# Attention heads of a hybrid decoder trunk: scaling and row minima inside the score instruction, a Newton step on ScalarE, fp32 sums of squares, and the second half of the keys' rows by DMA

## The chip, the cores and the metric

One NeuronCore of a Trainium2 chip runs the kernel: TensorE (PE) for matmuls, VectorE (DVE), ScalarE (ACT) and GpSimd (POOL) for elementwise work, SyncE (SP) for issuing most DMAs. Each engine works through its own queue in order and waits on semaphores for the others. The metric is device time in microseconds (us) of one execution; a comparison takes the median of several runs.

## The reference, cut to what matters

The trunk has one convolution layer, one differential-attention layer and a final RMSNorm, over 16 meta tokens and 1024 tokens of width 1024. All tensors are float32. The change lies in the attention layer, which has 8 heads, each with two query/key pairs of width 64 and values of width 128:

```python
for i in range(n_blocks):                       # blocks of 128 queries
    s = einsum("bqhmd,bkhmd->bhmqk", q[i], k[:qe]) * scale
    alibi = -slopes[:, None, None] * abs(qpos - kpos)
    s = where(valid, s + alibi[:, None], NEG_BIG)
    p = softmax(s, axis=-1)
    a = p[:, :, 0] - lam * p[:, :, 1]
    outs.append(einsum("bhqk,bkhe->bqhe", a, v))
o = rms_norm(o, subln_gain) * (1.0 - lambda_init)
o = o.reshape(b, l, DIFF_WIDTH) * silu(z)
return einsum("blc,cd->bld", o, w_out)
```

## The kernel before

The kernel keeps float32 accuracy on matmuls of a faster type: every operand is split into a high part (fp32r) and a low part, and a product is made of three passes, high by high, high by low and low by high. ACT casts the high part and DVE or POOL subtracts to get the low one (`lo_part`, L158). `passes` (L208) issues the matmuls of all projections.

The program runs in stages: norm, convolution with its two projections, second norm, values, then the eight heads, then the output projection and final norm. The order of each engine's instructions is not written by hand: a scheduler with a simulated timeline of its own sets it from the order of the code and the buffers that come free. So work of head h+1 (its projections `q`, `k` and `za`) stands between the attention work of head h on PE.

`queries(h)` makes `q2`: for each of the two pairs m, 64 rows of high parts and in the other 64 rows the low parts, so that one matmul of 128 rows gives both products with a key that stands twice. `keys(h)` therefore makes `k2[m]` and `kl2[m]` (high and low part of the keys, 1040 columns) with the same 64 rows in both halves: DVE scales the projection (`kt`, L889), ACT casts (L892), POOL subtracts (L158) and POOL copies both parts to the other 64 rows (L893 and L897), chunk by chunk (three chunks of some 347 columns).

`attention(h)` goes over four output quarters j of 256 queries, each of two blocks i of 128. For each block and each m the scores of up to 1040 keys come in one to three chunks: two matmuls into a score bank (L954, L955; three banks), then one DVE instruction (L957) that adds the distances `base`, writes `p` and gives the least value of the chunk to a column of `st`. The scores are held negated and divided by the head's slope. A DVE instruction or two (L962, L964, L968) take the least of the chunks and multiply by the slope; ACT then makes the exponential with scale -slope and that bias, and its row sum (L969); DVE the reciprocal (L973). For the second of the pair `st` is multiplied by -lambda (L976). ACT scales p0 (L982), DVE adds p1 times its factor (L983), PE transposes (L993), ACT and DVE split the result (L997, L998) and PE multiplies with the values into the one output bank `oo`.

Per quarter a norm follows: ACT squares the output (`osq`, L1023); for heads 0 to 3 (`SOH` = 4) the squares are split (L1028, `sr`) and summed by two fp32r matmuls with ones (L1031), for heads 4 to 7 by one fp32 matmul (L1033), into the second half of the output bank (`so`). ACT makes exp(-0.5 ln(so/128 + eps)) (L1035, L1036), DVE makes a Newton step for it (L1037, L1039, L1040, L1041), POOL one product (L1038); the result is split and stored by SP (`ya_d`).

SP's queue holds the loads of weights (`wf`, L174), those stores and, near the end of the heads, the loads of the residual (`f`, L1142), which go into buffers of the ring `qk` that held queries and keys of head 6. Work buffers of the norm (`sq`, `y`, `x`, `r`) come from a ring of four, `sm`.

## Time and profile before

| | us |
|---|---|
| median of 3 runs | 1518.32 |
| lowest and highest run | 1514.34, 1518.41 |
| the profiled execution's own time | 1522.14 |
| its span, first to last instruction | 1520.4 |
| PE busy in the span | 1430.9 (94%) |
| DVE busy | 1214.4 (80%) |
| POOL busy | 999.1 (66%) |
| ACT busy | 876.4 (58%) |

Busy time is a share over stages of different kinds, so one reads it by stretch. A matmul's record overlaps the next one's, so busy PE time includes some in which PE could have done more. In rows of groups the first number after the bar is busy time in us, the second the mean of one instruction in ns; behind the second bar stands the idle time of the engine just before such instructions and what ended it. In a row of a timeline or of the chain the first number is the start, the second the length.

### The profile page before, as it was taken

Reading aid. Unit: us, or ns where it says so; the run is one execution under the profiler, and the core shown is the slowest. Engines: PE = TensorE matmul, PEld = TensorE weight load, DVE = VectorE, ACT = ScalarE, POOL = GpSimd, SP = SyncE. Lnnn points to the kernel's source line nnn. Section 1 sums busy time; section 2 is a strip of 40 time slices with the busy share of each in tenths; the row PEclk is TensorE's granted clock in tenths of the full one; section 3 lists DMA queues with packets and bytes.
Section 4 is the critical chain, followed back from the end, with each engine's and each line's share of the span. In section 5 each row is a group of like instructions: output and inputs, shape, how many; then the busy total and the mean of one; then the engine's idle time right before and its main releaser. Section 6 shows DMA issues by size and latency. Waiting matters only on the chain.

```text
span 1520.4 us, 24170 instructions
## 1 busy us (share of the span) xinstructions
PE 1430.9 (94%) x8794; PEld 1332.9 (88%) x8794; DVE 1214.4 (80%) x2285; ACT 876.4 (58%) x1552; POOL 999.1 (66%) x782
## 2 busy tenths in 40 slices
PE   7799999999999988899999999989999999999887
PEld 6799999999999988799998878878888888887787
DVE  8999999989999988868445311689899898888784
ACT  5566666665655637546324412557768677687451
POOL 6599999999999973435014502947477485685572
PEclk9999999999999998899999999999999999999999
DMA  5021111112111313644453633111211212146541
GB/s 176 28 70 42 56 49 63 57 42 70 51 48 49 112 50 112 196 138 148 152 170 124 205 99 105 42 42 61 81 49 61 85 38 74 56 136 220 175 142 65
DMA packets 77369, 142.31 MB, mean 94 GB/s; under 512 B 6465, under 2 KB 45890, under 8 KB 76226
## 3 DMA queue, kind: packets, MB, share of 16 engines
q1 hardware_dynamic: 62242, 114.49, 23.1%
q0 software_dynamic: 5728, 17.04, 3.6%
q10 hardware_dynamic: 9280, 9.23, 1.8%
q8 instruction: 69, 1.13, 0.3%
q14 instruction: 50, 0.41, 0.1%
HBM read 106.73 MB, written 34.01 MB: 93 GB/s over the span
## 4 chain that ended last, share of the span: by engine, by line
PE 36%; DVE 24%; POOL 18%; ACT 10%; issue 8%; DMA 3%; SPq 0%; POOLq 0%; DVEq 0%; ACTq 0%
POOL pb L500 14%; PE c L208 8%; PE v L208 6%; PE z L208 5%; PE ao L208 3%; PE k L208 3%; PE u L208 3%; DVE p L957 3%; ACT pr L499 2%; DVE p L983 2%; ACT p L969 2%; PE q L208 2%; DVE v L534 2%; PE za L208 2%; PE g L208 1%
## 5 line engine op out<-in xcount | busy, mean ns | idle before, releaser
L500 POOL TENSOR_TENSOR pb<-pr,pb 128x521 f32<-128x521 f32 (+1 forms) x272 | 387.8, 1435 | 15.7 <-ACT pr L499 1.1
L499 ACT ACTIVATE pr<-vr,chn 128x521 f32<-128x521 f32 x224 | 150.7, 724 | 115.3 <-POOL pb L500 114.6
L208 PE MATMUL c<-b,wh 128*128 128x260 f32 x1024 | 190.5, 288 | 6.5 <-DVE b L158 3.9
L190 ACT ACTIVATE wh<-wf 128x1024 fp32r<-128x1024 f32 x115 | 121.0, 1052 | 105.7 <-PE c L208 51.3
L513 DVE SCALAR_TENSOR_TENSOR ev<-vr,chn,ev 128x520 f32<-128x520 f32 x240 | 180.7, 753 | 1.3
L208 PEld LDWEIGHTS c<-b,wh 128*128 128x128 f32 x1024 | 162.1, 193 | 7.7 <-DVE b L158 4.8
L208 PE MATMUL g<-hp,wh 128*128 128x346 f32 (+1 forms) x752 | 149.5, 329 | 13.7 <-DVE sig L467 6.0
L158 DVE TENSOR_TENSOR wl<-wf,wh 128x1024 fp32r<-128x1024 f32 x81 | 128.8, 1590 | 37.9 <-ACT wh L190 37.8
L208 PE MATMUL u<-hp,wh 128*128 128x346 f32 (+1 forms) x752 | 149.7, 321 | 3.5 <-ACT sz L432 2.1
L208 PE MATMUL c<-b,wl 128*128 128x260 f32 x512 | 146.5, 288 | 5.2 <-DVE wl L158 5.2
L969 ACT ACTIVATE p<-p,st 128x144 f32<-128x144 f32 (+7 forms) x128 | 100.5, 785 | 76.0 <-DVE st L964 41.8
L208 PEld LDWEIGHTS g<-hp,wh 128*128 128x128 f32 x752 | 125.8, 192 | 18.4 <-ACT n_r L233 6.3
L208 PE MATMUL z<-hp,wh 128*128 128x346 f32 (+1 forms) x768 | 136.2, 322 | 1.9 <-ACT sig L464 1.9
L513 DVE SCALAR_TENSOR_TENSOR od<-xs,wc,od 128x520 f32<-128x520 f32 x176 | 132.1, 751 | 0.0
L208 PEld LDWEIGHTS u<-hp,wh 128*128 128x128 f32 x752 | 124.5, 188 | 4.8 <-ACT sz L432 2.4
L208 PEld LDWEIGHTS z<-hp,wh 128*128 128x128 f32 x768 | 124.7, 189 | 2.7 <-ACT sig L464 2.2
L957 DVE CUSTOM_DVE_ANT_0 p<-s,total 128x144 f32<-128x144 f32 (+6 forms) x224 | 108.2, 500 | 13.1 <-PE s L955 10.0
L158 POOL TENSOR_TENSOR wl<-wf,wh 128x1024 fp32r<-128x1024 f32 x34 | 83.9, 2467 | 45.5 <-ACT wh L190 31.7
L208 PEld LDWEIGHTS c<-b,wl 128*128 128x128 f32 x512 | 98.8, 193 | 6.1 <-DVE wl L158 5.8
L667 POOL TENSOR_TENSOR total<-hsq,total 128x520 f32<-128x520 f32 x12 | 21.1, 1757 | 117.5 <-ACT hsq L666 117.5
L954 PE MATMUL s<-k,q 128*128 128x256 f32 (+6 forms) x224 | 76.8, 348 | 8.9 <-DVE st L957 8.7
L208 PE MATMUL z<-hp,wl 128*128 128x346 f32 (+1 forms) x384 | 74.2, 325 | 11.2 <-DVE wl L158 11.2
(300 smaller groups left out, 3723.2 us busy)
## 6 DMA issues: line engine op xcount, KB each, us to landing
wf<-conv_in SPq DMA_DIRECT2D x48, 512.0 KB, 3.4
wf<-conv_out SPq DMA_DIRECT2D x32, 512.0 KB, 3.8
wf<-attn_in SPq DMA_DIRECT2D x32, 512.0 KB, 3.5
wf<-attn_out SPq DMA_DIRECT2D x17, 512.0 KB, 3.5
sz_d<-sz ACTq DMA_DIRECT2D x32, 260.0 KB, 4.0
szr<-sz_d SPq DMA_DIRECT2D x16, 520.0 KB, 4.2
v<-v_d POOLq DMA_DIRECT2D x8, 1024.0 KB, 5.6
ya_d<-yb SPq DMA_DIRECT2D x28, 256.0 KB, 2.5
```

The costliest lines, as they stand in the source:

```text
L158: return eng.tensor_tensor(out=out_, in0=full, in1=hi, op=ALU.subtract)
L190: A.activation(out=wh, in_=wf, func=AF.Copy)
L208: PE.matmul(o, a[k], b[k], start=start and i == 0, stop=stop and i == tot - 1)
L499: A.activation(out=d, in_=src, func=AF.Copy, scale=w)
L500: G.tensor_tensor(out=dst, in0=d, in1=dst, op=ALU.add)
L513: V.scalar_tensor_tensor(out=dst, in0=src, scalar=w, in1=dst, op0=ALU.mult, op1=ALU.add)
L534: eng.tensor_tensor(out=v_t[i], in0=v_t[i], in1=mean, op=ALU.subtract)
L667: (V if SQA[m] == "V" else G).tensor_tensor(out=total[:, ns], in0=sq, in1=total[:, ns], op=ALU.add)
L954: PE.matmul(o[:, :wm], q2[m][:, qs], k2[m][:, c0 : c0 + wm], start=True, stop=False)
L957: V.tensor_tensor_reduce(out=p[:, c0 : c0 + w], in0=o[:, :w], in1=base[:, t0 + c0 : t0 + c0 + w], scale=1.0, scalar=0.0, op0=ALU.add, op1= ...
L969: A.activation(out=p[:, :n], in_=p[:, :n], func=AF.Exp, scale=-slope, bias=st[:, 0:1], accum_out=st[:, 1:2],)
L983: V.scalar_tensor_tensor(out=p0[:, :n], in0=p1[:, :n], scalar=s1[:, 3:4], in1=p0[:, :n], op0=ALU.mult, op1=ALU.add)
```

## The change

It touches only the heads.

- The score instruction takes the slope as its scale and, for the second and third chunk of a tile, the least value of the chunk before as its start value (3e38 for the first). So the last chunk's least value is that of the tile, already scaled, and the exponential uses scale -1 and it as bias. The small instructions in between are gone.
- The product with -lambda is a tensor_scalar with a scalar from memory in place of a tensor_tensor.
- In the Newton step, -0.5 so/128 - 0.5 eps is made by ACT (Identity with a bias tile), ACT squares r into a new buffer `rr` of the ring `sm`, and DVE multiplies once.
- `SOH` is 0: all heads sum the squares with one fp32 matmul.
- The keys' other 64 rows are written by four DMAs per head on SP's queue (64 x 1040 float32 each), issued after all three chunks, in place of POOL's copies per chunk.

```diff
@@ -60,7 +60,7 @@
 LOV = [(0, 2, 4, 6)] * 3
 SR = "G"
 SOE = "V"
-SOH = 4
+SOH = 0
 AGATE = [(7, 0)] * 3 + [(7, 1)] * 4
 AQ = "GGGGGGG"
 DIR0 = (False, False, False)
@@ -151,6 +151,8 @@
     V.memset(zero, 0.0)
     eps = gp.tile([P, 1], F32, name="eps")
     V.memset(eps, EPS)
+    half_eps = gp.tile([P, 1], F32, name="half_eps")
+    V.memset(half_eps, -0.5 * EPS)
     mod = gp.tile([P, KD, 3], F32, name="mod")
     sub_g = gp.tile([P, 1], F32, name="sub_g")
 
@@ -888,15 +890,14 @@
                 t = ev(f"kt{h}_{c0}")[:, :w]
                 V.tensor_tensor(out=t, in0=o, in1=rst[:, cs], op=ALU.mult)
                 for m in range(2):
-                    ms, other = slice(64 * m, 64 * m + 64), slice(64 - 64 * m, 128 - 64 * m)
+                    ms = slice(64 * m, 64 * m + 64)
                     A.activation(out=k2[m][ms, cs], in_=t[ms], func=AF.Copy)
-                    G.tensor_scalar(
-                        out=k2[m][other, cs], in0=k2[m][ms, cs].bitcast(F32), scalar1=1.0, scalar2=None, op0=ALU.mult
-                    )
                     lo_part(V if KL == "V" else G, kl2[m][ms, cs], t[ms], k2[m][ms, cs].bitcast(F32))
-                    G.tensor_scalar(
-                        out=kl2[m][other, cs], in0=kl2[m][ms, cs].bitcast(F32), scalar1=1.0, scalar2=None, op0=ALU.mult
-                    )
+
+            for m in range(2):
+                ms, other = slice(64 * m, 64 * m + 64), slice(64 - 64 * m, 128 - 64 * m)
+                for t in (k2[m], kl2[m]):
+                    SP.dma_start(out=t[other].bitcast(F32), in_=t[ms].bitcast(F32))
             return k2, kl2
 
         def gate(h):
@@ -947,33 +948,28 @@
                     for m in range(2):
                         p = pt(f"p{h}_{i}_{m}")
                         st = gp.tile([P, 8], F32, tag="stat", name=f"st{h}_{i}_{m}", bufs=6)
-                        mins = []
-                        for c0, w in even_chunks(n):
+                        least = 3e38
+                        for ci, (c0, w) in enumerate(even_chunks(n)):
                             wm = max(w, 256)
                             o = score(f"s{h}_{i}_{m}_{c0}")
                             PE.matmul(o[:, :wm], q2[m][:, qs], k2[m][:, c0 : c0 + wm], start=True, stop=False)
                             PE.matmul(o[:, :wm], q2[m][:, qs], kl2[m][:, c0 : c0 + wm], start=False, stop=True)
-                            mins.append(st[:, 4 + len(mins) : 5 + len(mins)])
+
                             V.tensor_tensor_reduce(
-                                out=p[:, c0 : c0 + w], in0=o[:, :w], in1=base[:, t0 + c0 : t0 + c0 + w], scale=1.0,
-                                scalar=0.0, op0=ALU.add, op1=ALU.min, accum_out=mins[-1],
+                                out=p[:, c0 : c0 + w], in0=o[:, :w], in1=base[:, t0 + c0 : t0 + c0 + w], scale=slope,
+                                scalar=least, op0=ALU.add, op1=ALU.min, accum_out=st[:, 4 + ci : 5 + ci],
                             )
-                        if len(mins) == 3:
-                            V.tensor_tensor(out=mins[1], in0=mins[1], in1=mins[2], op=ALU.min)
-                        if len(mins) > 1:
-                            V.tensor_scalar(
-                                out=st[:, 0:1], in0=mins[0], scalar1=mins[1], scalar2=slope, op0=ALU.min, op1=ALU.mult
-                            )
-                        else:
-                            V.tensor_scalar(out=st[:, 0:1], in0=mins[0], scalar1=slope, scalar2=None, op0=ALU.mult)
+                            least = st[:, 4 + ci : 5 + ci]
                         A.activation(
-                            out=p[:, :n], in_=p[:, :n], func=AF.Exp, scale=-slope, bias=st[:, 0:1],
+                            out=p[:, :n], in_=p[:, :n], func=AF.Exp, scale=-1.0, bias=least,
                             accum_out=st[:, 1:2],
                         )
                         V.reciprocal(out=st[:, 2:3], in_=st[:, 1:2])
                         pr.append((p, st))
                     (p0, s0), (p1, s1) = pr
-                    SMALL[SE].tensor_tensor(out=s1[:, 3:4], in0=s1[:, 2:3], in1=neg_lam, op=ALU.mult)
+                    V.tensor_scalar(
+                        out=s1[:, 3:4], in0=s1[:, 2:3], scalar1=neg_lam, scalar2=None, op0=ALU.mult
+                    )
                     if i in PSC:
                         G.tensor_scalar(
                             out=p0[:, :n], in0=p0[:, :n], scalar1=s0[:, 2:3], scalar2=None, op0=ALU.mult
@@ -1034,10 +1030,12 @@
                 x, r = small(f"ox{h}_{j}", w=256), small(f"or{h}_{j}", w=256)
                 A.activation(out=r, in_=so, func=AF.Ln, scale=1.0 / P, bias=eps)
                 A.activation(out=r, in_=r, func=AF.Exp, scale=-0.5)
-                V.tensor_scalar(out=x, in0=so, scalar1=-0.5 / P, scalar2=-0.5 * EPS, op0=ALU.mult, op1=ALU.add)
                 pool_ops[h, j] = G.tensor_tensor(out=y, in0=y, in1=r, op=ALU.mult).ins
-                V.tensor_tensor(out=x, in0=x, in1=r, op=ALU.mult)
-                V.tensor_tensor(out=x, in0=x, in1=r, op=ALU.mult)
+
+                A.activation(out=x, in_=so, func=AF.Identity, scale=-0.5 / P, bias=half_eps)
+                rr = small(f"rr{h}_{j}", w=256)
+                A.activation(out=rr, in_=r, func=AF.Square)
+                V.tensor_tensor(out=x, in0=x, in1=rr, op=ALU.mult)
                 V.scalar_tensor_tensor(out=y, in0=x, scalar=1.5, in1=y, op0=ALU.add, op1=ALU.mult)
                 if h == HEADS - 1 and j < 2:
                     if j == 0:

```

The scheduler sets a new order in the heads; up to there it is the same. Three places show it (line numbers of the changed kernel differ by a few from those before: its score instruction is L958, its key transfer L900). The first is DVE in head 3, around the seventh of eight blocks (`p3_6_0`, `p3_6_1`: probabilities of pair 0 and 1; `st`: their columns of least values, sums and factors). Before:

```order
L957 ISA p3_6_0_11730,st3_6_0_11731<-s3_6_0_456_11736,total_6321 128x456
L957 ISA st3_6_0_11731 128x1
L973 RECIPROCAL st3_5_1_11652<-st3_5_1_11652 128x1
L964 TENSOR_SCALAR st3_6_0_11731<-st3_6_0_11731 128x1
L976 TENSOR_TENSOR st3_5_1_11652<-st3_5_1_11652,neg_lam_8209 128x1
L983 SCALAR_TENSOR_TENSOR p3_5_0_11638<-p3_5_1_11651,st3_5_1_11652,p3_5_0_11638 128x784
L973 RECIPROCAL st3_6_0_11731<-st3_6_0_11731 128x1
L957 ISA p3_6_1_11743,st3_6_1_11744<-s3_6_1_0_11745,total_6321 128x456
L957 ISA st3_6_1_11744 128x1
L957 ISA p3_6_1_11743,st3_6_1_11744<-s3_6_1_456_11749,total_6321 128x456
L957 ISA st3_6_1_11744 128x1
```

Now:

```order
L958 ISA p3_6_0_11589,st3_6_0_11590<-s3_6_0_456_11595,total_6323,st3_6_0_11590 128x456
L958 ISA st3_6_0_11590 128x1
L994 TENSOR_TENSOR atl3_2_0_11460<-tp3_4_0_11490,ath3_2_0_11458 128x4x128
L958 ISA p3_6_1_11601,st3_6_1_11602<-s3_6_1_0_11603,total_6323 128x456
L958 ISA st3_6_1_11602 128x1
L994 TENSOR_TENSOR atl3_2_1_11461<-tp3_4_1_11497,ath3_2_1_11459 128x2x128
L958 ISA p3_6_1_11601,st3_6_1_11602<-s3_6_1_456_11607,total_6323,st3_6_1_11602 128x456
L958 ISA st3_6_1_11602 128x1
L967 RECIPROCAL st3_6_0_11590<-st3_6_0_11590 128x1
```

The multiplications with the slope (L964) are gone, and the second chunk's instruction reads `st`, which the first chunk's accumulator row wrote.

The second place is PE at the start of head 0, where the first scores (`s0_0_0_0`: head 0, block 0, pair 0) follow the key projection (`k0_2`); `q1_0` and `q1_1` are the two chunks of head 1's query projection. Before:

```order
L208 MATMUL k0_2_9138<-g7_8028,wl82_8358 128x346
L954 MATMUL s0_0_0_0_9181<-k0_0_9058,q0_0_8353 128x256
L208 MATMUL q1_0_9671<-g0_7172,wh83_9064 128x512
L208 MATMUL q1_0_9671<-g1_7293,wh83_9064 128x512
L954 MATMUL s0_0_1_0_9190<-k1_0_9059,q1_0_8354 128x256
L954 MATMUL s0_1_0_0_9208<-k0_0_9058,q0_0_8353 128x272
```

Now:

```order
L210 MATMUL q1_1_9666<-g1_7295,wh83_9066 128x512
L955 MATMUL s0_0_0_0_9175<-k0_0_9060,q0_0_8355 128x256
L210 MATMUL q1_1_9666<-g2_7417,wh83_9066 128x512
L210 MATMUL q1_1_9666<-g3_7540,wh83_9066 128x512
L955 MATMUL s0_0_1_0_9183<-k1_0_9061,q1_0_8356 128x256
L955 MATMUL s0_1_0_0_9200<-k0_0_9060,q0_0_8355 128x272
```

The first scores stood at place 5082, right behind the key projection; now they stand at 5116, behind 34 matmuls of head 1's query projection.

The third place is SP near the end of head 6 (`ya_d`: stores of finished quarters; `f`: residual loads; `wf`: weights). Before:

```order
L174 DMA wf105_14804<-attn_out 128x1024
L1052 DMA ya_d_8234<-yb5_3_13322 256x1x256
L1142 DMA f2_14783<-h1_d_76 128x1024
L1142 DMA f3_14784<-h1_d_76 128x1024
L1142 DMA f4_14785<-h1_d_76 128x1024
L1142 DMA f5_14786<-h1_d_76 128x1024
L1052 DMA ya_d_8234<-yb6_0_13661 256x1x256
```

Now:

```order
L1050 DMA ya_d_8236<-yb5_3_13128 256x1x256
L1050 DMA ya_d_8236<-yb6_0_13456 256x1x256
L1140 DMA f2_14545<-h1_d_78 128x1024
L1140 DMA f3_14546<-h1_d_78 128x1024
L900 DMA k0_7_13903<-k0_7_13903 64x1040
L900 DMA k1_7_13904<-k1_7_13904 64x1040
L1140 DMA f4_14547<-h1_d_78 128x1024
L900 DMA kl0_7_13905<-kl0_7_13905 64x1040
L900 DMA kl1_7_13906<-kl1_7_13906 64x1040
L176 DMA wf106_14595<-attn_out 128x1024
```

The four transfers of head 7's keys stand behind the first two residual loads and around the third; on PE, 23 matmuls of the gate projection, 19 of head 6's output and 8 transposes stand between head 6's last score matmul and head 7's first.

## Rows read from the trace of the kernel before

**Rows 1.** Stretches of the heads: start and end, length, busy time by engine, PEclk, DMA

```profile
943.00:1029.70 86.70, 80.87 (x462) 72.02 (x461) 60.16 (x195) 51.61 (x115) 62.68 (x61) 0.98 0.13 40
1029.70:1389.70 360.00, 345.54 (x2017) 306.67 (x2017) 320.98 (x939) 257.90 (x548) 245.04 (x239) 0.99 0.26 86
1389.70:1430.00 40.30, 36.27 (x179) 30.07 (x179) 36.29 (x90) 27.24 (x49) 17.61 (x15) 0.96 0.40 123
```

**Rows 2.** Timeline of ACT, one load per head: start, length, instruction

```profile
1029.74 1.28 ACT L911 ACT_TABLE_LOAD   x1
...
1389.74 1.28 ACT L911 ACT_TABLE_LOAD   x1
```

**Rows 3.** Chain of waits, from 900 to 1440 us: start, length, engine, tile, line

```profile
899.89 35.06 PE v L208 x151
938.62 11.42 PE k L208 x72
...
1311.54 0.87 PE tp L993 x8
```

**Rows 4.** What PE waited for, 943 to 1430 us: total, times, longest

```profile
PE s L954 <- DVE st L957: 8.7, 9, 3.9
PE tp L993 <- DVE p L983: 5.0, 2, 3.9
```

**Rows 5.** Groups of DVE, 943 to 1430 us: busy time and mean, then idle before

```profile
L976 DVE TENSOR_TENSOR st<-st,neg_lam 128x1 f32<-128x1 f32 x64 | 22.6, 354 | 1.1
...
L1040 DVE TENSOR_TENSOR ox<-ox,or 128x256 f32<-128x256 f32 x29 | 18.1, 624 | 0.4
...
L964 DVE TENSOR_SCALAR st<-st 128x1 f32<-128x1 f32 x80 | 16.5, 206 | 0.7
...
L1037 DVE TENSOR_SCALAR ox<-o 128x256 f32<-128x256 f32 x30 | 12.5, 417 | 1.8 <-ACT or L1035 1.6
...
L158 DVE TENSOR_TENSOR sr<-osq,sr 128x256 fp32r<-128x256 f32 x16 | 9.3, 580 | 0.0
...
L968 DVE TENSOR_SCALAR st<-st 128x1 f32<-128x1 f32 x48 | 6.1, 146 | 0.3
```

**Rows 6.** Groups of POOL and ACT, whole span

```profile
L897 POOL TENSOR_SCALAR kl<-kl 64x346 fp32r<-64x346 f32 (+1 forms) x48 | 57.3, 1193 | 4.0
...
L893 POOL TENSOR_SCALAR k<-k 64x346 fp32r<-64x346 f32 (+1 forms) x48 | 55.9, 1166 | 7.2 <-ACT k L892 4.3
...
L1035 ACT ACTIVATE or<-o,eps 128x256 f32<-128x256 f32 x32 | 14.7, 459 | 2.0 <-PE o L1033 1.6 <-PE o L1031 0.3
...
L1036 ACT ACTIVATE or<-or 128x256 f32<-128x256 f32 x32 | 13.1, 408 | 0.3
```

**Rows 7.** Timeline of DVE and POOL, at 1247 and 1415 us

```profile
1247.09 1.08 POOL L897 TENSOR_SCALAR kl<-kl 64x346 fp32r<-64x346 f32 x1
...
1247.86 1.30 DVE L983 SCALAR_TENSOR_TENSOR p<-p,st,p 128x1040 f32<-128x1040 f32 x1
...
1415.53 3.97 DVE L1039 TENSOR_TENSOR ox<-ox,or 128x256 f32<-128x256 f32 x1
...
1416.85 2.35 POOL L158 TENSOR_TENSOR wl<-wf,wh 128x1024 fp32r<-128x1024 f32 x1
```

**Rows 8.** Timeline of PE around a sum of squares in fp32

```profile
1361.20 0.39 PE L208 MATMUL za<-g,wl 128*128 128x512 f32 x1
...
1362.33 0.59 PE L1033 MATMUL o<-osq,ones 128*128 128x256 f32 x2
1362.57 0.59 PE L208 MATMUL za<-g,wl 128*128 128x512 f32 x1
```

**Rows 9.** DMA issues from 900 to 1440 us: times, KB each, median us to landing

```profile
v<-v_d POOLq DMA_DIRECT2D x8, 1024.0 KB, 5.6
...
ya_d<-yb SPq DMA_DIRECT2D x28, 256.0 KB, 2.5
...
f<-h_d SPq DMA_DIRECT2D x8, 512.0 KB, 4.5
```

## The prediction

> **What bounds the kernel now.** I read the stretches of the span first, with each engine's busy time in each, because the change touches only the heads. The eight heads fill 943 to 1430 us. In the six steady head periods from 1029.7 to 1389.7 us TensorE (PE) is busy 345.5 of 360.0 us and VectorE (DVE) 321.0; ScalarE (ACT) and GpSimd (POOL) are at 257.9 and 245.0 [rows 1]. The reader is to see two engines near their end at once. The buffers between them are shallow here (three score banks, one output bank), so a late DVE is soon a late PE.
>
> PE's busy time hides part of its slack, since records of matmuls overlap. So I made PE's work per head from pace. One table load of ACT marks each head's gate: 1029.74 and, six heads later, 1389.74 us, so a head takes 60.0 us [rows 2]. The chain of waits has stretches in which PE only streams: 151 matmuls of 512 columns in 35.06 us (0.232 us each, 0.4535 ns a column), 72 of a key projection in 11.42 us, 8 transposes in 0.87 us [rows 3]. A head has 96 matmuls of 512 columns (22.3 us), 72 for keys (11.4), scores of 19,392 columns (8.8), 64 of 256 for the output (7.4), 44 transposes (4.8) and 8 of 256 for the sums (0.9): 55.6 us. The slack is 4.4 us a head, 26.4 us in the six periods. No change on the other engines can give back more than that there.
>
> Who ends PE's waits? Between 943 and 1430 us PE's page idle is 5.8 + 14.5 + 4.0 = 24.3 us [rows 1], and its two largest waits, 13.7 us, end on DVE: the score instruction that frees a bank, and the difference p0 - lambda p1 ahead of the transposes [rows 4]. So relief of DVE goes to the right place, and PE's slack limits what it brings.
>
> **The change part by part.** *DVE, removed.* The small instructions after the scores, L964 (80 x 0.206 us = 16.5) and L968 (6.1) go (and L962, 16 times, which I leave uncounted), since the score instruction now scales and carries the least value along. The product with -lambda, L976, falls from 0.354 us to that of a one-column form with a scalar from memory, 0.206: 64 x 0.148 = 9.5. The Newton step loses L1037 (12.5) and one of two products; I take the cheaper one, L1040 (18.1). The low part sr of heads 0 to 3 goes: 9.3 [rows 5]. The sum is 72.0 us.
>
> *DVE, added.* 96 of the 224 score instructions (the second and third chunks of a tile) now read the least value that the instruction ahead of them has just written, and wait for it. No row shows that. Bounds: 0, and 0.206 us each (the whole of a small instruction, 19.8 us). I take the difference between L964, which reads a scalar from memory, and L968, which has it in the instruction: 0.06 us, 5.8 in all, because such a wait falls beside the score bank's own. Behind the waiting instruction stand the rest of DVE's queue, and ACT's exponential. Net relief: 66 of DVE's 417.4 us, 16%.
>
> *ACT.* Two instructions more per quarter: a linear one from PSUM (as L1035, 0.459) and a square (as L1036, 0.408): 32 x 0.867 = 27.7 us [rows 6]. ACT goes from 336.8 to about 364 of 487 us, 75%, and waited for DVE before; I count nothing on the path (bounds 0 to +3, if a tile's exponential comes behind them). The output bank is now released by ACT, which has the linear one right behind the logarithm.
>
> *POOL.* L893 and L897 go: 55.9 + 57.3 = 113.2 us of 325.3 [rows 6]. POOL was not what PE waited for, so this alone is worth 0; its cover is the low parts and weight parts that POOL still makes.
>
> Whether DVE gets faster beside an emptier POOL is the first doubtful place. One row has DVE's L1039 at 3.97 us beside a POOL subtraction, where L1040, of the same shape, has a mean of 0.62 [rows 5, 7]. The other pair has L983 starting 0.31 us before POOL's L897 ends and done in 1.30 us for 1040 columns: at most 0.31 us lost to a copy [rows 7]. So it is the subtractions that hold DVE, and they stay; I count no gain for the copies (bounds 0 and 96 x 0.31 = 30 us of DVE). The Trainium skill, SBUF — State Buffer, section Who interferes with whom, says that a DVE instruction with two SBUF inputs and a GpSimd instruction that reads SBUF exclude each other, and the one that starts later waits wholly. By it the removal of a third of POOL's work would take a third of DVE's such waits away, which the second pair of rows leaves open only up to 0.31 us each; the rival in which everything opens is what that would give.
>
> *PE.* Heads 0 to 3 sum squares with one fp32 product of two passes in place of two fp32r products. In the row of a later head the pair is recorded at its own pace, but the next matmul takes 0.59 us where its like took 0.39 [rows 8]: 0.2 us more, 16 x 0.2 = 3.2 us, all on PE (bounds 0 and 3.2).
>
> *DMA.* 32 new transfers of 64 rows, 266 KB each, on SP's queue. At the start of head 0 PE reaches the first scores 34 matmuls later than before (the order), 7.9 us at 0.232. A 256 KB store lands in 2.5 us, a 1 MB load in 5.6 [rows 9]; key projection ends at 938.62 + 11.42 = 950.0, the last low parts some 4 us later (DVE's kt, ACT's k, POOL's two subtractions behind a weight part: an estimate), and the low products are a further 11 projection matmuls off, so arrival falls at 957 to 960 and use at about 960.5: cost 0, bounds 0 and +3. In heads 1 to 6 over 80 matmuls lie between: 0. In head 7 the key transfers stand behind two residual loads that wait for head 6's last scores; PE has 23 large matmuls, 19 of 256 columns and 8 transposes in between, 8.4 us, against five issues and a landing of 4.5 us [rows 9]. I take +1, bounds 0 and +6.
>
> The Trainium skill, SBUF — State Buffer, section Door 1: The DMA port swizzle, says that 64 rows reach no more DMA ports than 32 do, at 196 GB/s for 1 MiB; by it the four transfers of a head take an estimated 5.4 us and not the time of 128 rows, which would add 1 to 3 us to the head 7 term. The 5.6 us row already covers that, so the sum stays.
>
> **Sum.** I take two thirds of the steady slack, -17.6, because most of PE's waits end on DVE but the exponential's own latency remains; half of the first stretch's idle 5.8, -2.9, because head 0's softmax starts later; and -5 in the last 40.3 us, where DVE is busy 36.3 (between PE's idle 4.0 and DVE's share, 16% of 36.3 = 5.8). With +3.2 and +1 this is -21.3. The profiled execution took 1522.14 us (span 1520.4), so 1500.8 there. The median of the runs shown is 3.8 us lower; the same step gives **1497 us**.
>
> **The rivals.** *PE is the bound already (18%).* Steady periods hardly move, as PE's 345.5 of 360 would say; only first and last stretch gain, 7.9 less 4.2: 1514.6, or 1512 with a tenth of the steady slack. Against it: the pace count, and that the waits end on DVE.
>
> *Everything opens (14%).* The whole slack goes: -26.4 - 5.8 - 5.8 + 3.2 = -35, 1483. DVE's waits beside POOL would have to go as well, the 30 us of the bound above. For it: 3.97 us in one instruction; against it: the pair with 1.30. The rule of exclusion named above would favour this one.
>
> *The keys come late (9%).* SP's queue is in order; a key transfer waits for POOL's low parts, and stores and weight loads stand between. If the halves land after PE has reached a head's first scores, PE stands still microsecond for microsecond, in eight heads. Nothing happens up to the margins above; at 3 us a head the gain is eaten, and 4 us gives 32 - 21 = +11, 1529. For it: the 8.4 us of head 7; against: 80 matmuls elsewhere.
>
> *The relief is not there (3%).* If each chained score instruction costs far more than its bound of 0.206, 0.75 us, the 96 of them eat all that was removed: 1518.
>
> **How the numbers follow.** My case (1490 to 1510) has 56%. About 0.3%, from 1513.8 to 1522.9, is what a measurement can tell. Half of the first rival lies below that: faster 0.56 + 0.14 + 0.09 = 0.79, same 0.09 + 0.03 = 0.12, slower 0.09. The range leaves out the best part of the second rival and the third: 1480 to 1517.
>
> **What would show it.** Right: no head period above 59 us between table loads, DVE near 350 us in sum over the heads, PE's waits on the score bank cut by half, L1040 and L964 gone. Wrong: PE waiting for a transfer of k or kl; score instructions of the second chunk longer than 0.06 us over the first; DVE still over 85% busy; ACT's exponential behind the new square; periods at 60 us with PE's pace full.

## The result, and the profile after

The changed kernel takes 1495.54 us (median of 4 runs, 1494.0 to 1498.89) beside 1518.12 us of the kernel before (4 runs, 1514.34 to 1518.41): ratio 0.9853, 95% interval 0.9834 to 0.9872, 22.6 us less. The forecast was 1497 us. The profiled execution took 1494.0 us (span 1492.2), 28.1 us less than that of before; 3.9 us of this lie ahead of the first change, where the two programs are the same, so I compare from PE's last value matmul on: 572.3 us before, 548.1 after, 24.2 us less. One execution, the profiled one of e_dve_in_chain below, took 2803 us and is left out everywhere.

To split this I don't use the table loads of [rows 2], since the planner (the scheduler with the simulated timeline) put them elsewhere among the matmuls. I cut both traces where PE has done the same amount of streaming (start-to-start pace of each kind of matmul, taken from all runs); another measure of the pace moves a cut by about 1 us, in e_newton_only by 3. First before, then after; the columns are those of [rows 1].

```profile
938.23:1029.49 91.26, 85.43 (x490) 76.69 (x489) 61.17 (x196) 52.71 (x117) 64.35 (x63) 0.98 0.16 49
1029.49:1389.53 360.04, 345.58 (x2017) 306.56 (x2017) 321.02 (x940) 257.94 (x548) 244.87 (x239) 0.99 0.26 86
1389.53:1510.50 120.97, 111.33 (x707) 99.48 (x705) 86.27 (x162) 59.07 (x107) 62.48 (x49) 0.97 0.39 125
```

```profile
934.29:1019.82 85.53, 83.57 (x487) 75.46 (x486) 53.20 (x159) 51.99 (x115) 36.23 (x37) 1.00 0.27 77
1019.82:1371.37 351.55, 340.37 (x2014) 306.04 (x2015) 269.25 (x766) 275.32 (x588) 162.25 (x168) 1.00 0.35 108
1371.37:1482.36 110.99, 108.56 (x712) 97.68 (x711) 77.17 (x148) 59.31 (x114) 61.54 (x49) 1.00 0.41 131
```

The reader is to see three things. With nearly the same matmuls (the count behind PE's busy time) the stretches are 5.7, 8.5 and 10.0 us shorter, so the middle gave least for its length; PE's idle time (length less busy) fell by 3.9, 3.3 and 7.2 us, its busy time by the rest. DVE's busy time fell by 69 us (468.5 to 399.6), POOL's by 112. And the granted clock, third from the end of each row (0.98, 0.99, 0.97), is 1.00 in all three now: that was in no term of mine.

What PE waits for in the heads (939 to 1404 us; total, times, longest), beside [rows 4]:

```profile
PE ao L210 <- DMA a<-ya_d: 5.0, 5, 1.4
PE s L955 <- DVE st L958: 3.7, 3, 1.8
PE s L956 <- DMA kl<-kl: 2.6, 2, 2.2
```

The wait on the score bank is 3.7 us where it was 8.7, its longest 1.8 where it was 3.9, and the wait of the transposes for the difference (5.0) is gone. New are the waits for the key transfers, and that for the loads a (normed output of earlier heads, read back) was 1.9. The groups of DVE, each shape apart, that answer to [rows 5]: first chunks and chained ones of the same width, and the product with -lambda.

```profile
L958 DVE CUSTOM_DVE_ANT_0 p<-s,total,st 128x456 f32<-128x456 f32 x16 | 11.0, 685 | 0.3
L958 DVE CUSTOM_DVE_ANT_0 p<-s,total 128x456 f32<-128x456 f32 x16 | 9.9, 622 | 0.2
...
L958 DVE CUSTOM_DVE_ANT_0 p<-s,total,st 128x346 f32<-128x346 f32 x16 | 9.1, 571 | 0.7
...
L958 DVE CUSTOM_DVE_ANT_0 p<-s,total 128x346 f32<-128x346 f32 x16 | 8.2, 510 | 0.5 <-PE s L956 0.5
...
L970 DVE TENSOR_SCALAR st<-st,neg_lam 128x1 f32<-128x1 f32 x63 | 13.2, 210 | 1.4
```

A chained score instruction takes 0.06 us more than a first one (685 against 622 ns, 571 against 510).

### The profile page after: what moved, and what is told of

The parts are those of the page before. It is cut to its first block, busy times and chain, and to the rows that moved or that the text cites. A ratio compares the mean times of both kernels' runs of the same rounds, so it can differ in the third digit from the quotient of the medians.

```text
span 1492.2 us, 24057 instructions
## 1 busy us (share of the span) xinstructions
PE 1421.2 (95%) x8794; PEld 1331.1 (89%) x8794; DVE 1146.7 (77%) x2062; ACT 893.9 (60%) x1600; POOL 886.3 (59%) x686
## 4 chain that ended last, share of the span: by engine, by line
PE 58%; POOL 13%; DVE 13%; issue 6%; ACT 5%; DMA 4%; SPq 0%; DVEq 0%; POOLq 0%; ACTq 0%
POOL pb L502 11%; PE c L210 7%; PE v L210 6%; PE z L210 6%; PE q L210 5%; PE k L210 5%; PE za L210 5%; PE u L210 5%; PE ao L210 4%; PE g L210 3%; PE o L210 3%; PE s L955 2%; PE s L956 2%; PE tp L989 2%; DVE v L536 2%
## 5 line engine op out<-in xcount | busy, mean ns | idle before, releaser
L192 ACT ACTIVATE wh<-wf 128x1024 fp32r<-128x1024 f32 x115 | 121.1, 1053 | 112.6 <-PE c L210 58.9
L963 ACT ACTIVATE p<-p,st 128x272 f32<-128x272 f32 (+7 forms) x128 | 100.4, 785 | 36.0 <-DVE st L958 35.3
L210 PE MATMUL v<-wv,g 128*128 128x512 f32 x352 | 83.5, 394 | 0.0
L210 PE MATMUL g<-hp,wl 128*128 128x346 f32 (+1 forms) x376 | 81.4, 321 | 0.0
```

Of the source, the lines that this page charges most:

```text
L192: A.activation(out=wh, in_=wf, func=AF.Copy)
L210: PE.matmul(o, a[k], b[k], start=start and i == 0, stop=stop and i == tot - 1)
L963: A.activation(out=p[:, :n], in_=p[:, :n], func=AF.Exp, scale=-1.0, bias=least, accum_out=st[:, 1:2],)
```

## Where the two largest waits of before came from

Both waits of 3.9 us in [rows 4] have one DVE instruction in front of them. The timeline of the kernel before around the first wait, at 1011 us, and around a like place at 997 us (start, length, instruction; in brackets the idle time and what ended it):

```profile
997.20 2.38 POOL L158 TENSOR_TENSOR wl<-wf,wh 128x1024 fp32r<-128x1024 f32 x1
997.31 2.28 DVE L976 TENSOR_TENSOR st<-st,neg_lam 128x1 f32<-128x1 f32 x1
...
1011.52 2.34 POOL L158 TENSOR_TENSOR wl<-wf,wh 128x1024 fp32r<-128x1024 f32 x1 [4.33 <-ACT p L969]
...
1011.65 2.22 DVE L976 TENSOR_TENSOR st<-st,neg_lam 128x1 f32<-128x1 f32 x1
...
1015.69 1.11 PE L993 MATMUL tp<-ident,p 128*128 128x128 f32 x4 [3.93 <-DVE p L983]
...
1420.58 0.42 PE L954 MATMUL s<-k,q 128*128 128x346 f32 x1 [3.91 <-DVE st L957]
```

All instances of L976 (shortest, median and longest in ns):

```profile
L976 DVE TENSOR_TENSOR st<-st,neg_lam x64: 141/159/2283, 962.8 to 1427.6; 128x1 f32<-128x1 f32 x64
```

A product of one column takes 2.2 us and ends when POOL's subtraction ends: 997.31 + 2.28 = 999.59 beside 997.20 + 2.38 = 999.58, and 1013.87 beside 1013.86. Then comes the difference, then PE. The other wait is the pair of [rows 7] at 1415: L1039 lasts until 1419.50, 0.30 us after POOL's subtraction ends, and PE starts again at 1420.58 after 3.91 us; that L1039 was held already for 1.3 us before the subtraction's recorded start isn't explained. So the mean of 0.354 us of L976 in [rows 5] was not its form: its median is 0.159 us, and 64 x (0.354 - 0.159) = 12.5 us of it, as an estimate, were time behind POOL. The new form is slower when free (0.21 us) and never held: its 64 instances lie between 0.19 and 0.22 us. The Trainium skill, SBUF — State Buffer, section Who interferes with whom, says that a DVE instruction with two SBUF inputs and a GpSimd instruction that reads SBUF exclude each other; these rows agree with it for POOL's subtractions.

A stop of this kind costs PE more than its length. Before, around the second one (the columns of [rows 1], four microseconds a row), and after, around its longest run of short stops:

```profile
1414.00:1418.00 4.00, 2.67 (x16) 2.01 (x15) 4.00 (x2) 1.80 (x4) 3.98 (x5) 1.00 0.57 151
1418.00:1422.00 4.00, 1.42 (x6) 1.33 (x7) 4.00 (x10) 0.00 (x0) 1.20 (x1) 0.93 0.98 302
1422.00:1426.00 4.00, 4.00 (x14) 3.14 (x14) 3.35 (x15) 2.89 (x5) 0.00 (x0) 0.64 0.28 83
```

```profile
1361.00:1365.00 4.00, 2.50 (x18) 1.94 (x16) 1.72 (x8) 1.67 (x6) 1.10 (x2) 1.00 1.15 389
1365.00:1369.00 4.00, 2.83 (x7) 2.25 (x8) 1.61 (x5) 3.96 (x5) 0.00 (x0) 0.60 1.10 389
```

Before, PE is idle for 2.6 of four microseconds, and then, fully busy again, does 14 matmuls at a granted clock of 0.64: part of that row is at the lower level of 1.2 GHz. I added up (1 - granted clock) x length over rows of 5 us below 0.99: before 8.6 us, in five places (1013, 1093, 1153, 1418, 1473 us), after 1.7, in one. So up to 6.9 of the 24.2 us are clock (all of it, if PE would have streamed all the time). The Trainium skill, TensorE: Matmul & The Clock Gate, section What's actually happening, says that the clock follows how busy PE has been; the rows agree.

This doesn't hang on one execution, since every run has its granted clock on record. (1 - granted clock) x span, which includes the stages ahead, has a mean of 28.9 us over 65 runs of the kernel before and 22.8 over the four of the changed one; a mean of four is good to about 2 us.

## The experiments

In the table, "heads on" is the time from PE's last value matmul to its last matmul, "clock" the sum just described, both of the profiled run; the ratio is to runs of the kernel before taken beside each kernel, with its 95% interval. Their medians were 1519.5 us beside the four single parts, 1517.9 beside the four that put work back, 1518.1 beside the pinned ones and 1518.6 beside n_keys_first, so differences between rows go by the ratios.

| kernel | median us | ratio | heads on | three stretches | clock |
|---|---|---|---|---|---|
| before | 1518.1 | | 572.3 | 91.3, 360.0, 121.0 | 8.6 |
| after | 1495.5 | 0.9853 (0.9834 to 0.9872) | 548.1 | 85.5, 351.5, 111.0 | 1.7 |
| e_scores_only | 1510.8 | 0.9943 (0.9926 to 0.9960) | 562.8 | 89.7, 358.8, 114.3 | 6.7 |
| e_newton_only | 1517.6 | 0.9991 (0.9978 to 1.0004) | 567.6 | 90.2, 356.4, 121.0 | 8.5 |
| e_dma_only | 1514.3 | 0.9968 (0.9954 to 0.9981) | 564.7 | 85.2, 368.3, 111.2 | 1.8 |
| e_sums_only | 1514.6 | 0.9964 (0.9950 to 0.9977) | 566.8 | 87.4, 358.4, 121.1 | 6.8 |
| e_pool_copies | 1508.7 | 0.9936 (0.9914 to 0.9958) | 560.1 | 88.1, 353.3, 118.7 | 6.8 |
| e_idle_copies | 1495.1 | 0.9846 (0.9826 to 0.9866) | 547.6 | 86.5, 345.9, 115.2 | 5.1 |
| e_dve_beside | 1494.0 | 0.9841 (0.9821 to 0.9860) | 545.2 | 85.5, 344.4, 115.3 | 1.7 |
| e_dve_in_chain | 1494.4 | 0.9842 (0.9822 to 0.9861) | | | |
| p_copies_order_after | 1523.5 | 1.0034 (1.0022 to 1.0045) | 574.2 | 93.8, 369.1, 111.3 | 15.4 |
| p_before_order_after | 1526.5 | 1.0045 (1.0028 to 1.0062) | 574.8 | 95.5, 363.1, 116.2 | 3.4 |
| p_after_order_before | 1520.7 | 1.0011 (1.0001 to 1.0021) | 572.7 | 94.9, 358.1, 119.7 | 15.5 |
| n_keys_first | 1495.7 | 0.9852 (0.9833 to 0.9871) | 545.9 | 85.5, 349.1, 111.3 | 1.7 |

### One part alone

My theory was that DVE's busy time is the price (A); the rivals were the latency ahead of the exponential (B) and POOL's copies slowing DVE (C). The scores, in the kernel before:

```diff
-                                out=p[:, c0 : c0 + w], in0=o[:, :w], in1=base[:, t0 + c0 : t0 + c0 + w], scale=1.0,
-                                scalar=0.0, op0=ALU.add, op1=ALU.min, accum_out=mins[-1],
+                                out=p[:, c0 : c0 + w], in0=o[:, :w], in1=base[:, t0 + c0 : t0 + c0 + w], scale=slope,
+                                scalar=least, op0=ALU.add, op1=ALU.min, accum_out=st[:, 4 + ci : 5 + ci],
...
-                            out=p[:, :n], in_=p[:, :n], func=AF.Exp, scale=-slope, bias=st[:, 0:1],
+                            out=p[:, :n], in_=p[:, :n], func=AF.Exp, scale=-1.0, bias=least,
```

> The kernel before with the score part alone: slope and running least value inside the score instruction, the exponential with scale -1, and the product with -lambda in the one-column form. It takes 22.6 + 9.5 - 5.8 = 26 us off DVE. Theory A, DVE's busy time is what counts (the whole change took 66 us off DVE for about 26 us of time before the 3 us of the fp32 sums are paid, 0.39 us per us): -10 us, 1508. Theory B, what counts is the latency from the last score to the exponential, which only this part shortens (one small instruction less, 128 times): -15 to -20 us, nearly the whole gain. Theory C, POOL's copies are what slowed DVE: -3 us or less. In A and B, DVE's small instructions L962, L964 and L968 are gone and the chained score instructions take 0.06 us more than first ones of their width.

The Newton step:

```diff
-                V.tensor_scalar(out=x, in0=so, scalar1=-0.5 / P, scalar2=-0.5 * EPS, op0=ALU.mult, op1=ALU.add)
...
-                V.tensor_tensor(out=x, in0=x, in1=r, op=ALU.mult)
-                V.tensor_tensor(out=x, in0=x, in1=r, op=ALU.mult)
...
+                A.activation(out=x, in_=so, func=AF.Identity, scale=-0.5 / P, bias=half_eps)
+                rr = small(f"rr{h}_{j}", w=256)
+                A.activation(out=rr, in_=r, func=AF.Square)
+                V.tensor_tensor(out=x, in0=x, in1=rr, op=ALU.mult)
```

> The kernel before with the Newton step alone: linear term and square on ACT. It takes 30.6 us off DVE and puts 27.7 on ACT. Theory A (DVE's busy time): -12 us, 1506. Theory B (latency ahead of the exponential): -2 to -5 us, since the norm of a quarter is not between scores and exponential. Theory C (POOL's copies): -3 us or less.

The key transfers in place of POOL's copies:

```diff
-                    G.tensor_scalar(
-                        out=k2[m][other, cs], in0=k2[m][ms, cs].bitcast(F32), scalar1=1.0, scalar2=None, op0=ALU.mult
-                    )
...
+                for t in (k2[m], kl2[m]):
+                    SP.dma_start(out=t[other].bitcast(F32), in_=t[ms].bitcast(F32))
```

> The kernel before with the keys' other rows by four DMAs a head in place of POOL's copies, and nothing else. POOL loses 113 us. Theories A and B: 0, between -3 and +4 us. Theory C (the copies slow DVE by their reads, up to 0.31 us each): DVE's busy time over the heads falls by 15 to 30 us and the time by 6 to 12 us. Keys that come late would show as PE waits for DMA at the first scores of a head and +3 us or more.

The fp32 sums:

```diff
-SOH = 4
+SOH = 0
```

> The kernel before with fp32 sums of squares in all heads. DVE loses 9.3 us (sr), POOL nothing, PE gains some 3.2 us of streaming by the 0.2 us a pair. Theory A: -3.6 + 3.2, about 0. Theory B: 0 to +3. If the fp32 pair costs PE nothing, -4.

By the intervals the scores save 6 to 11 us, the key transfers 3 to 7, the sums 3.5 to 8, and the Newton step saves 3 or costs 1 at most. The medians add up to 20.7 us; together the parts brought 22.6. No theory holds in all four. Theory A has the scores right (-10, measured -8.7) and the Newton step wrong (-12, measured -2): that step took 35 us off DVE (434 against 468 us in "heads on"), the sums took 10 off and brought more. Part of this is clock: over its runs (1 - granted clock) x span is 32.6 us with the Newton step alone and 29.8 in the kernel before beside it, and without these 2.8 us the step brings about 4.

The transfers, worth 0 to me, brought 5, and that is clock: up to 6.8 of their 7.6 us in "heads on", and over all runs 23.6 us of clock against 29.8. Theory C's sign on DVE came true, though. Before, and with the transfers alone (DVE is the third busy time):

```profile
938.23:1510.50 572.27, 542.35 (x3212) 482.73 (x3210) 468.45 (x1296) 369.72 (x769) 371.70 (x350) 0.99 0.27 89
935.75:1500.43 564.68, 537.87 (x3211) 478.38 (x3210) 449.93 (x1296) 368.92 (x769) 260.46 (x254) 1.00 0.34 105
```

DVE's busy time fell by 18.5 us, within the 15 to 30 expected, and the time by less than the 6 to 12. Little of it is the copies' own hold: of DVE's instructions in the kernel before, those that met a copy and nothing else on POOL lasted at most 0.32 us longer than the shortest of their kind, 4.3 us in all. The rest are meetings with subtractions, which the new order set otherwise.

### Back into the changed kernel

Four kernels put work back. The copies on POOL instead of the transfers, the diff of the key transfers above read backwards:

> The changed kernel with POOL's copies of the key rows put back in place of the four DMAs a head. POOL gets 113 us of work back. My theory (POOL is not waited for): the time of the changed kernel, 1495.5, within 3 us. Rival (copies slow DVE or come late for PE): 1501 to 1508, with DVE's busy time over the heads up by 15 to 30 us.

The same copies as idle work; nothing reads them, and the keys still come by transfer:

```diff
+                        G.tensor_scalar(
+                            out=t[other], in0=part[ms, cs].bitcast(F32), scalar1=1.0, scalar2=None, op0=ALU.mult
+                        )
```

> The changed kernel with the same 96 copies on POOL put back as idle work: they go to rows of a scratch tile that nothing reads, and the keys still come by DMA. This prices POOL's load without the keys' path. My theory: 1495.5, within 3 us. Rival (contention of POOL's copies with DVE): 1501 to 1508, DVE's mean durations up. If this stays and the run with real copies is slower, it is the keys' path through POOL and not the load.

An unused DVE instruction per tile, and then the same one between the last score and the exponential:

```diff
+                        V.tensor_scalar(out=st[:, 0:1], in0=least, scalar1=neg_lam, scalar2=None, op0=ALU.mult)
```

> The changed kernel with one unused DVE instruction of one column (about 0.2 us) behind the last score instruction of each of the 128 tiles: 26 us of DVE work are back, and ACT's exponential does not read its result. Theory A (DVE's busy time counts, 0.39 us per us): +10 us, 1505. Theory B (only the latency ahead of the exponential counts): 0 to +3 us. Theory D (PE is the bound now at 95% busy and DVE has room): 0 to +2 us.

```diff
-                            out=p[:, :n], in_=p[:, :n], func=AF.Exp, scale=-1.0, bias=least,
+                        V.tensor_scalar(out=st[:, 0:1], in0=least, scalar1=ones[:, 0:1], scalar2=None, op0=ALU.mult)
+                            out=p[:, :n], in_=p[:, :n], func=AF.Exp, scale=-1.0, bias=st[:, 0:1],
```

> The same extra instruction, but the exponential takes its bias from it, so 0.2 us more lie between the last score and the exponential, 128 times. Theory A: the same as the run with the unused instruction, +10 us. Theory B: +10 to +20 us, clearly above that run. Theory D: 0 to +4 us for both.

The idle copies cost nothing, with POOL's 113 us all back. The 128 unused instructions cost nothing, and neither do they in the chain (ratio 0.9842, 0.9822 to 0.9861). So in the changed kernel neither 21 us of DVE's busy time nor 0.2 us of latency ahead of the exponential shows in the time, as theory D has it. But each of these kernels also has an order of its own, which shifts more than that between the stretches (344.4 and 115.3 us in e_dve_beside, 351.5 and 111.0 in after), so the load isn't priced apart from the order. Only the real copies cost, 13 us. Of the 12.0 us in "heads on", up to 5.1 are clock (6.8 against 1.7); 7.7 lie in the last stretch, and there the timeline shows one stop:

```profile
1420.47 2.93 POOL L1144 DMA_DIRECT2D a<-ya_d  x4
1420.92 0.43 DVE L1040 SCALAR_TENSOR_TENSOR ya<-ox,ya 128x256 f32<-128x256 f32 x1
...
1422.24 6.12 DVE L160 TENSOR_TENSOR y<-ya,y 128x256 fp32r<-128x256 f32 x1 [0.29 <-ACT y L1048]
1423.42 2.37 POOL L160 TENSOR_TENSOR wl<-wf,wh 128x1024 fp32r<-128x1024 f32 x1
1425.74 2.33 POOL L160 TENSOR_TENSOR wo_at<-wf,wo_at 128x1024 fp32r<-128x1024 f32 x1
...
1428.42 0.79 PE L210 MATMUL af<-y,wh 128*128 128x512 f32 x1 [4.25 <-DVE y L160]
```

A subtraction of 256 columns starts while POOL issues four loads, and ends at 1428.36, after POOL's next two subtractions (1428.07). PE waits 4.25 us, and the row from 1427 to 1431 has a clock of 0.59. The load issues alone hold nothing: another DVE instruction of that size with two inputs in SBUF ran among them in 0.43 us (at 1420.92). Why the held one stood from before the subtraction's recorded start is not shown. The copies aren't part of these rows; that they shifted what meets what is the likely reading. The last stretch goes by such meetings in all kernels: the longest DVE instruction in it, up to 1460 us, is 3.97 us in before, 4.57 with the Newton step alone, 6.49 with the sums alone, 6.12 here and 6.14 in p_after_order_before, and the stretch has 118.7 to 121.1 us; it is at most 2.5 us in after, with the transfers alone and in p_copies_order_after, and the stretch has 111. The others lie between, at 114 to 116 us, some with one of 4 us and some with none over 2.6, so the length alone doesn't decide. What the copies cost in the other two stretches, 2.6 + 1.8 us, is not shown apart from the clock.

### Order against work

The planner writes a new order for every kernel: PE's program in the heads is the same in after, e_pool_copies and e_sums_only, but a matmul stands some four to five places elsewhere on average, up to 87. So I pinned one kernel's order on another's work, by edges that set the order of issue and nothing else. The first of three kernels pins PE, DVE and ACT; the other two pin PE alone, and the planner orders the other engines around it. The edges themselves cost nothing: n_keys_first below pins all four engines to the changed kernel's own order and takes its time, 1495.7 us.

```diff
+        for a, b in zip(places, places[1:]):
+            tc.add_manual_dep(traced[b], traced[a].name, dep, reason="pin")
```

> POOL's real key copies in the changed kernel, as in the run that took 1508.7 us, but with the order of PE's, DVE's and ACT's instructions in the heads pinned to that of the changed kernel (edges that set only the order of issue, no waits). Theory E, the order that the planner wrote is what the copies spoiled (PE's matmuls stand 5 places elsewhere on average, up to 87, though the program is the same): 1495 to 1499. Theory F, the keys' own path through POOL makes PE wait: 1505 or more, with PE waits for POOL at scores. A tie at half of each: 1500 to 1504.

> The kernel before with fp32 sums (so that PE's program is the same, 1514.6 us) and PE's order of the heads pinned to the changed kernel's; all of the old DVE, ACT and POOL work is there. Theory E (order): most of the 19 us between the two comes with the order: 1497 to 1504. Theory A (relief of DVE, ACT's and POOL's part): the order alone is worth less than a third, 1508 to 1515, or it is worse than 1515, because the old work cannot follow it.

> The changed kernel with PE's order of the heads pinned to that of the kernel before with fp32 sums. Theory E (order): 1507 to 1515, the gain goes. Theory A (relief): 1495 to 1501, the gain stays in another order.

All three are slower than the kernel before, the third only just, and no theory holds in all of them. The real copies in the new order took more than 1505, as theory F has it, but its sign, PE waiting for POOL at the scores, didn't come. The old work in the new order is worse than 1515, which theory A allowed, "because the old work cannot follow it". The new work in the old order loses the gain, as theory E has it, and 6 us more than its range. With PE's program equal, the table is (medians, in brackets the ratio to the kernel before)

| | PE's order of before (fp32 sums) | PE's order of after |
|---|---|---|
| work of before (fp32 sums) | 1514.6 (0.9964) | 1526.5 (1.0045) |
| work of after | 1520.7 (1.0011) | 1495.5 (0.9853) |

By the ratios either half alone loses 7 to 12 us; both together gain 17. So what the order brings and what the relief brings can't be told apart by adding: an order suits the work that it was planned for. The rows show where the time goes. The old work in the new order (PE's waits, 939 to 1430 us) is late on POOL, at `cor` (a copy of 16 rows that the last product of a quarter reads), and on DVE:

```profile
PE o L1020 <- POOL cor L1007: 12.4, 4, 3.6
PE s L954 <- DVE st L957: 7.6, 8, 2.1
```

The new work in the old order stops at the first scores of head 0, which stand 34 matmuls earlier there, for the transfer of the keys, and again in the last stretch:

```profile
952.03 0.55 PE L955 MATMUL s<-k,q 128*128 128x256 f32 x1 [4.63 <-DMA k<-k]
...
1435.00 6.14 DVE L1039 SCALAR_TENSOR_TENSOR ya<-ox,ya 128x256 f32<-128x256 f32 x1
...
1441.65 1.22 PE L210 MATMUL af<-y,wh 128*128 128x512 f32 x2 [5.85 <-ACT y L1047]
```

Each stop is followed by low clock (0.50 from 953 to 957 us and from 1440 to 1444), up to 15.5 us in all. PE's waits aren't shorter with the lighter work in the old order. First the old work (e_sums_only), then the new:

```profile
938.34:1505.18 566.84, 540.56 (x3211) 481.33 (x3210) 458.14 (x1280) 366.32 (x753) 369.57 (x350) 0.99 0.27 89
935.59:1508.34 572.75, 543.32 (x3212) 486.71 (x3210) 407.30 (x1072) 388.48 (x817) 259.70 (x254) 0.97 0.34 103
```

PE is idle for 26.3 us in the one and 29.4 in the other. The real copies under the new order have the two kinds of stops of the old work there (10.8 us for POOL's `cor`, 11.8 for DVE's score instruction, 15.4 us of clock).

### The end of the heads

In the changed kernel's queue of SP the residual loads f stand among the last head's key transfers. n_keys_first moves them behind, with the other four engines' orders pinned to those of after:

```diff
+            with tc.issue_after(key_dma[last]):
+                SP.dma_start(out=f_t[m], in_=h1_d[m, :, META:])
```

> The changed kernel with one thing moved: in SP's queue the residual loads f stand behind head 7's four key transfers (PE's, DVE's, ACT's and POOL's orders are pinned to those of the changed kernel, so only SP's queue differs, in 8 places). In the trace of the changed kernel the keys of head 7 take 8 to 11 us to land among 512 KB loads, PE waits 2.6 us for kl and 5.0 us for the loads a behind it. Theory G, the residual loads crowd the keys: the 2.6 us go and part of the 5.0, 1490 to 1493.5. Theory H, the loads a alone fill the transfers' time, or the wait only moves to a or to f: 1494 to 1497. Slower than 1497 would mean that the residual loads now come late for the sums that read them.

The landing times from 900 to 1440 us in after (KB, median us), and what PE waits for from 1325 to 1380 us in n_keys_first:

```profile
a<-ya_d POOLq DMA_DIRECT2D x14, 512.0 KB, 8.0
k<-k SPq DMA_DIRECT2D x16, 260.0 KB, 3.8
kl<-kl SPq DMA_DIRECT2D x16, 260.0 KB, 5.1
f<-h_d SPq DMA_DIRECT2D x8, 512.0 KB, 12.2
```

```profile
PE ao L210 <- DMA a<-ya_d: 4.7, 3, 2.6
PE s L958 <- DMA kl<-kl: 1.1, 1, 1.1
```

The wait for kl falls from 2.6 to 1.1 us, that for a stays. "Heads on" is 2.2 us shorter, all of it in the middle stretch, which holds this place (349.1 against 351.5); the first stretch is 85.5 us in both. The median is the same as that of after: PE's last value matmul starts at 936.7 us in this profiled run and at 934.3 in that one, with equal code ahead, so 2 us are below what the total tells. Theory G in the heads, theory H in the time; no version beat the changed kernel by more than that.

## Why the prediction was right, and where not

*The sum* was -21.3, against -24.2 us in the profiled runs and -22.6 in the medians. That it came so near is luck in part: its terms erred both ways.

*DVE, removed and added:* right in sum. From [rows 1] with the loads as marks DVE was to fall from 417 to about 350 us; it fell to 347.1 (52.3, 267.2 and 27.6). The chained instruction costs the 0.06 us taken. The product with -lambda fell as forecast, for another reason than the form (above).

*The slack* was counted too small. Between the two table loads stand 554 matmuls of 512 columns (288 of `za`, 240 of `q`, 26 of `ao`), not 6 x 96 = 576, so by the same pace it is some 31.5 us and not 26.4.

*What DVE's relief is worth* is the step that failed, "two thirds of the steady slack", -17.6. It took DVE's load as the price and the steady periods as the place. The middle stretch gave 8.5 us where that term, less the two small costs, was 13.4; the first gave 5.7 (forecast 2.9), the last 10.0 (forecast 5). The errors nearly cancel. The Newton step alone shows 35 us of DVE worth 3 at most, about 4 without the clock, and the unused instructions show 21 us (420 against 400) worth nothing, each in an order of its own.

What counted in the first and last stretch were a few long stops, where one DVE instruction was held behind POOL and PE stood behind it, and the clock after them: waits of PE over 1.5 us were 11.7 us there (four) and are 1.8 (one), and up to 5.1 us are clock. In the middle there was no such stop before: 14.1 us in 22 shorter waits became 7.2 in ten and 3.9 in two long ones, and up to 1.7 us are clock. Another 3.5 us of the middle are shorter busy time of PE, and their cause stays open.

*The clock* was in no term: up to 6.9 us of the profiled pair, some 6 over all runs.

*Contention with POOL:* I concluded from [rows 7] that subtractions hold DVE and copies don't. Nearly so: a copy alone costs an instruction 0.32 us at most, and the idle copies add 8 us to DVE's 400 and nothing to the time. But I then counted no gain, though the change takes away DVE instructions that the subtractions held: L976 alone 12.5 us, one of its instances right ahead of a wait of 3.9 us.

*POOL, 0:* the load is worth 0 in the changed kernel, as said. The swap itself brought 5 us alone, which over all runs is the clock, and I had no term for it.

*The fp32 sums, +3.2:* wrong in sign. Alone they bring 3.5 to 8 us. PE's start-to-start time at these sums, the waits behind them included, is 12.9 us before and 9.2 after; the 0.59 us of [rows 8] was one row.

*The transfers:* head 0 costs 0, as said, but only because the order puts 34 matmuls ahead; in the old order it is 4.6 us. Heads 1 to 6 show no wait. Head 7, +1 (0 to 6): the waits for kl and a there are 7.6 us, where the wait for a was 1.9 before, so 5.7, near the upper end; part of it is the crowding by the residual loads, which land in 12.2 us where it was 4.5 [rows 9]. A 260 KB transfer of 64 rows lands in 3.8 to 5.1 us, where a 256 KB store took 2.5 [rows 9]. The Trainium skill, SBUF — State Buffer, section Door 1: The DMA port swizzle, says that 64 rows reach half as many ports as 128, and this agrees in direction. That the four transfers of a head run at the same time, which may lengthen the landing too, isn't told apart.

*The rivals:* "PE is the bound already" was wrong of the kernel before and fits the kernel after, with the planner's order as part of the bound. "The keys come late" happened in head 7 alone, and in head 0 in the pinned order. "Everything opens" and "the relief is not there" didn't happen. Of the signs of being wrong, one showed: PE waits 2.6 us for kl. The period between loads has a mean of 57.5 us, as wanted, but the last is 61.2, over the 59 named, and part of the mean is the mark: by equal work it is 351.5 / 6 = 58.6.

## What to carry to other kernels

Don't price relief of a second engine by its busy time. Look for the waits of the bounding engine, the few long ones first, find the one instruction behind each, and add the clock of the microseconds after. Where a planner writes the order, a change of work is a change of order too; pinning shows how much hangs on the two suiting each other. Compare stretches of equal work from a mark in the trace, since with one order those repeat (85.5 us twice) where the total varies by 2 to 4 us.

## What the runs showed of the hardware

- A DVE product of one column was held 2.2 us until POOL's subtraction ended, and one subtraction of 256 columns 6.1 us, over the end of POOL's four load issues and two subtractions in a row. A DVE instruction of that size ran in 0.43 us among the same issues.
- POOL's copies with a scalar, 96 of them, changed neither the time nor, by more than 8 of 400 us, DVE's busy time. A DVE instruction that met a copy alone took at most 0.32 us longer.
- Stops of PE of 3.9 to 5.9 us were followed by a granted clock of 0.50 to 0.78 in the row of four microseconds in which they end or the next one; one order had up to 15.5 us of low clock, another 1.7.
